# Order of the last weight loads in a fused decoder kernel: two down parts ahead of the embedding's gate weights, and a split emitted later

## The chip, the cores and the metric

The kernel runs on one core of a Trainium2 chip. Five engines of the core matter: PE (matrix products; its weight loads are listed as PEld), DVE and ACT (elementwise work), POOL (little here) and SP, which only issues transfers. Each engine works through its own queue of instructions in order; semaphores tie the queues together. The metric is the time of one execution in microseconds (us) on the device. "Slower" and "faster" are measured against the kernel before, on the same chip.

## The reference, cut to what matters

Two layers are computed for 256 tokens of width 1024 in float32. The last sub-layer of the second layer and what follows it are these lines:

```python
y = jnp.zeros(xf.shape, F32)
for e in range(N_EXPERTS):                       # 8 experts, top 2 of 8 for each token
    y = y + combine[:, e:e + 1] * swiglu(xf, w_gate_up[e], w_down[e]).astype(F32)
...
x = layer_norm(DEEPNORM_ALPHA * x + h, ln_ffn_g[i], ln_ffn_b[i])     # h is y
x = x + jax.nn.sigmoid(x @ ple_w_gate[i]) * (p[i] @ ple_w_proj[i])   # the gated embedding
```

An expert has 1024 x 7168 weights for gate and up and 3584 x 1024 for down, 44 MB in all; the eight make 352 MB. `ple_w_gate` has 4 MB for a layer, `ple_w_proj` 1 MB.

## The kernel before

**Experts.** `experts` goes over eight turns `e`, one expert each, sorted by how many tokens they got. Turn `e` handles `GR[e]` groups of 32 tokens; the last turn, 7, has two groups. The hidden width is cut into four quarters `q`. `gate_up(e, q)` makes a quarter's hidden values (eight tiles of weights of 1 MB; the last quarter is half as wide and has four), ACT and DVE apply the gate, `trans(e, q)` turns them (`hT`), and `down(e, q)` multiplies them with the down weights (four tiles of 1 MB; two for the last quarter). `down(e, q - 1)` stands behind `gate_up(e, q)`, so the last piece of the text is `gate_up(7, 3)`, `down(7, 2)`, `trans(7, 3)`, `down(7, 3)`. `trans(7, 3)` writes `hT`, which `down(7, 3)` reads.

**Ring.** Every weight tile is one turn of a ring of 22 buffers of 1 MB (`ringtile`, L785). `TURNS = "3p4p5p6p7ppp21089abcxx"` names the buffer of each turn: a digit or a to c is a buffer with its own tag, `p` is any of seven buffers that share one tag, `x` any of two that share another. The turn in `Finish.load` that takes `self.pw` is a first letter of the string. A turn waits until the work that read the buffer 22 turns before is done.

**The end.** `Finish` (L1233) does what follows the experts. `load` takes tiles for `ple_w_proj` (`pw`), for the split of p (`pTs`), and for the four pieces of `ple_w_gate` (`raws`; called gate loads 1 to 4 below), and issues these five loads. `prepare` splits a float32 weight into a high part (a cast on ACT) and a low part (a subtraction on DVE): twice for `pw`, twice for p (source `pT1`, made at the start of the experts' stage), and eight times for `raws` (called gate casts 1 to 8; two for each gate load). Between them stand the 24 products `p_part` of p with `ple_w_proj` on PE, which ACT copies away (`pp`). It also loads the norm's two vectors (`gb`). `end` gathers the last expert's result (`collect`), places and adds it, normalises, turns, and multiplies with the gate weights; it sends the output.

**Order.** The queues are laid down when the program is built, by a planner that plays the program through a model of the engines and the loads. Whenever an engine is free there, it takes the first instruction in the text that can begin; later text may overtake text that waits. Two things bind it. Inside `in_order` (all of `end`) an engine keeps the order of the text. And the tiles of one tag are handed out in the order in which their first writes stand in the text, also where a buffer would be free earlier. Tags that matter here: the seven `p` buffers, and `mis`, four banks of PSUM (`psM`), of which the last expert's sum holds one from `down(7, 0)` on, and of which `p_part`, `trans(7, 3)` and the turn of the placement matrix (`scatter`) take one each time they call `mis()`.

In the trace nearly every instruction carries line 90, the helper that records it; groups are told apart by the tiles' names. All ring tiles are named `raw`.

Of the kernel before, what the change touches and what calls it, by code (L numbers as in the profile page):

```python
# [19 lines left out]
P = 128  # L20
S = 256
D = 1024
NB = S // P
DFF = 2816
NE = 8
# [49 lines left out]
def trunk(ctx: ExitStack, tc: tile.TileContext, cst, x, p, ln_mix_g, ln_mix_b, ln_ffn_g, ln_ffn_b, ab_w_in,  # L75
          ab_b_f, ab_w_out, c_w_qkv, c_sinks, c_w_out, ffn_w_gate_up, ffn_w_down, router_w, router_b,
          moe_w_gate_up, moe_w_down, ple_w_gate, ple_w_proj, out):
    nc = tc.nc
# [50 lines left out]
    def mis():  # L129
        return psM.tile([P, 512], F32, tag="mis", name="mis")  # L130
# [44 lines left out]
    def rawtile(dt=F32):  # L175
        return rawp.tile([P, 2048], dt, tag="raw", name="raw", bufs=7)
# [163 lines left out]
    def p_part(prep, b, n, ac):  # L340
        pT, HL = prep
        for k in range(2):
            for j, (a, w) in enumerate(((0, 0), (0, 1), (1, 0))):
                T.matmul(ac, pT[b][:, a, k, :], HL[k][w][:, 512 * n:512 * (n + 1)],
                         start=(k == 0 and j == 0), stop=(k == 1 and j == 2))
        return ac
# [438 lines left out]
    def ringtile(dt=F32):  # L785

        i = TURNS[turn[0] % len(TURNS)]
        turn[0] += 1
        if i == "p":
            return rawtile(dt)  # L790
        if i == "x":
            return big.tile([P, 2048], dt, tag="xT", name="raw", bufs=2)
        return ring.tile([P, 2048], dt, tag="raw" + i, name="raw", bufs=1)
# [34 lines left out]
    def fetch_(dst, src):  # L828
        with after(queued[0]):
            queued[0] = nc.sync.dma_start(dst, src)  # L830
# [5 lines left out]
    def of_turn(w, e, static):  # L836

        if static or e == 0:
            return w[0, e]
        if not ids:  # L840
            for i in range(1, NE):
                with after(queued[0]):
                    ids[i] = nc.values_load(idi[0:1, i:i + 1], engines=[mybir.EngineType.SP], min_val=0, max_val=NE - 1)
        return w[0, bass.ds(ids[e], 1)].rearrange("o d f -> (o d) f")

    def load_gu(dst, e, q, k, s=slice(0, 2), static=False):
        wgu = of_turn(moe_w_gate_up, e, static).rearrange("(k p) (s n) -> p k s n", p=P, s=2)
        fetch_(dst, wgu[:, k, s, cols[q]])
# [7 lines left out]
    for b in range(NB):  # L856
# [5 lines left out]
        for k in range(8):  # L862
            q = T.matmul(ps[0:NE, 0:P], rw[:, k, :], t[:, 0, k, :], start=(k == 0), stop=(k == 7))
# [117 lines left out]
    def experts(rest, finish):  # L981
# [6 lines left out]
        items, raws = [], {}  # L988
# [3 lines left out]
                if e or q:  # L992
                    items += [(e - (q == 0), (q - 1) % 4, k) for k in range(chunks[q - 1])]
        items += [(NE - 1, 3, k) for k in range(chunks[3])]
        used, passed = [0], [None]

        def fetch(e, q, k, s=None):
            if s is None:
                if k % 2 == 0:
                    raws[0] = raw = ringtile()  # L1000
                    wd = of_turn(moe_w_down, e, rest).rearrange("(k p) n -> p k n", p=P)
                    step = 1 if e == NE - 1 and q == 3 and k == 2 else 2
                    for i in range(0, 2, step):
                        fetch_(raw[:, D * i:D * (i + step)].rearrange("p (k n) -> p k n", n=D),
                               wd[:, 8 * q + k + i:8 * q + k + i + step, :])
                return raws[0][:, D * (k % 2):D * (k % 2 + 1)]
            if q == 3:
                if k % 2 == 0:
                    raws[2] = t = ringtile()
                    for i in range(2):  # L1010
                        load_gu(t[:, D * i:D * (i + 1)].rearrange("p (s n) -> p s n", s=2), e, q, k + i, static=rest)
                return raws[2][:, D * (k % 2):D * (k % 2 + 1)]
            if s == 0:
                raws[2] = ahead.pop((q, k), None) if not rest and e == 0 else None
                if raws[2] is None:
                    raws[2] = ringtile()
                    load_gu(raws[2].rearrange("p (s n) -> p s n", s=2), e, q, k, static=rest)
            return raws[2][:, FQ * s:FQ * (s + 1)]

        def weights(*it):  # L1020
            assert items[used[0]] == it
            used[0] += 1
            return fetch(*it)

        def place_of(dst, e, b, n):

# [113 lines left out]
        def down(e, q):  # L1140
            n = gr[e]
            m = 2
            if q == 0:
                st[e]["y"] = [mis() for _ in range((n + 1) // 2)]
            y = [(st[e]["y"][g // 2][:, 256 * (g % 2):256 * (g % 2 + 1)], g % 2 == 0) for g in range(n)]
            hT = st[e]["hT%d" % q]
            for k in range(chunks[q]):
                W = weights(e, q, k)
                mm = side_by_side(y, [hT[:, g * m + k % m, k // m, :] for g in range(n)], W,
                                  q == 0 and k == 0, q == 3 and k == chunks[3] - 1)  # L1150
                if k == min(KT, chunks[q] - 1):
                    passed[0] = mm
# [8 lines left out]
        def ystile():  # L1161
            return moe.tile([P, D], F32, tag="ys", name="ys", bufs=1)
# [38 lines left out]
        for e in range(NE):  # L1201
            for q in range(4):
                gate_up(e, q, dict(zip(SC, scatter(e - 1))) if q == 1 and e else {})
                if not rest and e == 0 and q == 0:
                    gates()
                    turn_p()
                if not rest and e == 0 and q == 2:
                    gather((1,), xs)
                    keep_x()
                if e == NE - 1 and q == 3:  # L1210
                    finish.load()
                    finish.prepare()
                if q:
                    down(e, q - 1)
                elif e:
                    down(e - 1, 3)
                if q == 3 and e % 2 and e + 1 < NE:
                    gather((e + 1, e + 2), xk)
                trans(e, q)
                if e == NE - 1 and q == 3:  # L1220
                    scatter(e)[0](None)
        down(NE - 1, 3)
        ys = ystile()
        finish.end(functools.partial(collect, st[NE - 1]["y"], ys, gr[NE - 1]), ys, st[NE - 1]["pT"], CT * gr[NE - 1],
                   functools.partial(add, NE - 1))
# [3 lines left out]
    def turn_p():  # L1229
        for b in range(NB):  # L1230
            A.copy(pT1[:, b], tr4(pt1[:, b], 2)[:, :2 * P].rearrange("p (k t) -> p k t", t=P))

    class Finish:  # L1233


        def load(self):
            self.pw, self.pTs = ringtile(), ringtile(F32R)
            nc.sync.dma_start(self.pw.rearrange("p (k n) -> p k n", n=D), ple_w_proj[1].rearrange("(k p) n -> p k n", p=P))
            w = ple_w_gate[1].rearrange("(k p) n -> p k n", p=P)
            self.raws = []  # L1240
            for n in range(2):
                for k0 in (0, 4):
                    self.raws.append(ringtile())
                    nc.sync.dma_start(self.raws[-1].rearrange("p (k n) -> p k n", n=512),
                                      w[:, k0:k0 + 4, 512 * n:512 * (n + 1)])

        def parts(self, t, src):

            split(t[:, :D], t[:, D:], src)
            return t[:, :D], t[:, D:]  # L1250

        def prepare(self):

            pHL = [self.parts(ringtile(F32R), self.pw[:, D * k:D * (k + 1)]) for k in range(2)]
            pTs = self.pTs[:, :8 * P].rearrange("p (b a k t) -> p b a k t", b=NB, a=2, k=2)
            for b in range(NB):
                split(pTs[:, b, 0], pTs[:, b, 1], pT1[:, b])
            self.pp = ringtile().rearrange("p (b n) -> p b n", b=NB)
            for b in range(NB):
                for n in range(2):  # L1260
                    A.copy(self.pp[:, b, half[n]], p_part(([pTs[:, i] for i in range(NB)], pHL), b, n, mis()))
            self.HL = [[], []]
            for i in range(8):
                H, L = self.parts(ringtile(F32R), self.raws[i // 2][:, D * (i % 2):D * (i % 2 + 1)])
                for k in range(2):
                    sl = slice(512 * k, 512 * (k + 1))
                    self.HL[i // 4].append((H[:, sl], L[:, sl]))
            self.gb = ringtile()
            for i, v in enumerate((ln_ffn_g, ln_ffn_b)):
                nc.sync.dma_start(self.gb[:, D * i:D * (i + 1)], v[1:2, :].broadcast_to([P, D]))  # L1270
            x2t = ringtile().rearrange("p (b n) -> p b n", b=NB)
            self.x2 = [x2t[:, b, :] for b in range(NB)]
            self.xT = [ringtile(F32R).rearrange("p (a k t) -> p a k t", a=2, k=8) for b in range(NB)]
# [109 lines left out]
```

## Time and profile before

| what | value |
|---|---|
| runs (3) | 1373.24, 1374.14, 1376.18 us; median 1374.14 |
| the profiled execution | 1376.53 us, of it 1374.8 us from the first to the last instruction (the span) |
| busy PE / DVE / ACT / POOL | 1345.0 / 396.1 / 326.7 / 27.5 us |
| HBM read | 430.21 MB |

A row of a timeline has the start, the duration, the engine, the line, the operation, the tiles written and read, the shapes, the number of instructions, and in brackets the idle time of the engine before and what ended it. PE records two instructions for each float32 product with expert weights, so that one tile of down weights of the last turn makes 32. PEclk is the granted TensorE clock, 1.00 for 2.4 GHz and 0.50 for 1.2 GHz. All times in rows are counted from the span's start.

### The profile page before, as it was taken

How to read it: one execution, taken by the hardware profiler on the slowest of the kernel's cores; microseconds unless marked ns; L12 is line 12 of the kernel's file. 1: busy time of each engine (PE TensorE's matmuls, PEld its weight loads, DVE VectorE, ACT ScalarE, POOL GpSimd, SP SyncE). 2: the span in 40 equal slices, each digit the busy share in tenths (PEclk: the TensorE clock that was granted, in tenths of full speed). 3: DMA queues.
4: the chain of work that ended last, by engine and by line, in shares of the span. 5: the costliest groups of instructions: out<-in, count | busy, mean ns of one | idle time of the engine just before them, and what ended most of it. 6: DMA issues, size and time to landing. Idle time of an engine off the chain costs nothing. (4 is left out here: it accounts for less than half of the span.)

```text
span 1374.8 us, 37450 instructions
## 1 busy us (share of the span) xinstructions
PE 1345.0 (98%) x16967; PEld 891.3 (65%) x16967; DVE 396.1 (29%) x781; ACT 326.7 (24%) x618; POOL 27.5 (2%) x31
## 2 busy tenths in 40 slices
PE   8999999999999999999999999999999999999977
PEld 6786788888776666655556555665555665665546
DVE  5466654555877700010010011001010002002054
ACT  4545444443557100110010010011010001001041
POOL 0000300000000000000000000000000000000000
PEclk9999999999999999999999999999999999999988
DMA  9462564566581899999999999999999999999950
GB/s 323 160 204 74 162 204 138 168 223 198 174 325 68 318 403 405 384 399 400 408 408 401 407 407 392 407 406 392 407 408 395 399 408 406 389 408 407 377 224 34
DMA packets 143146, 433.77 MB, mean 316 GB/s; under 512 B 8834, under 2 KB 14978, under 8 KB 142978
## 3 DMA queue, kind: packets, MB, share of 16 engines
q1 hardware_dynamic: 142834, 431.22, 82.4%
q8 instruction: 135, 2.21, 0.7%
q14 instruction: 33, 0.27, 0.1%
q10 hardware_dynamic: 144, 0.07, 0.0%
HBM read 430.21 MB, written 1.05 MB: 314 GB/s over the span
## 5 line engine op out<-in xcount | busy, mean ns | idle before, releaser
L90 PE MATMUL acc<-raw,xg 128*32 128x256 f32 x9408 | 519.7, 380 | 0.0
L90 PEld LDWEIGHTS acc<-raw,xg 128*32 128x32 f32 x9408 | 300.9, 110 | 209.7 <-issue 11.3
L90 PE MATMUL mis<-raw,hT 128*32 128x256 f32 x4704 | 262.7, 379 | 2.1 <-DMA raw<-in_moe_w_down 2.1
L90 PE MATMUL acc<-H,xT 128*128 128x512 f32 (+2 forms) x768 | 227.8, 380 | 0.8 <-ACT xT L90 0.8
L90 DVE TENSOR_TENSOR h<-h,acc 128x512 f32<-128x512 f32 (+2 forms) x64 | 37.8, 596 | 638.1 <-PE acc L90 478.9
L90 PEld LDWEIGHTS mis<-raw,hT 128*32 128x32 f32 x4704 | 151.8, 110 | 103.7 <-DMA raw<-in_moe_w_down 2.7
L90 DVE TENSOR_TENSOR L<-raw,H 128x1024 fp32r<-128x1024 f32 (+2 forms) x134 | 151.2, 1135 | 110.2 <-ACT H L90 109.6
L90 ACT CAST H<-raw 128x1024 fp32r<-128x1024 f32 (+2 forms) x138 | 133.6, 975 | 147.4 <-PE acc L90 136.9
L90 PEld LDWEIGHTS acc<-H,xT 128*128 128x128 f32 x768 | 141.1, 192 | 29.0 <-ACT xT L90 1.7
L90 ACT ACTIVATE h<-acc 128x512 f32<-128x512 f32 (+2 forms) x64 | 32.9, 522 | 482.8 <-PE acc L90 482.8
L90 PE MATMUL acc<-L,xT 128*128 128x512 f32 (+2 forms) x384 | 141.3, 374 | 0.0
L90 PEld LDWEIGHTS acc<-L,xT 128*128 128x128 f32 x384 | 72.6, 189 | 13.8 <-DVE L L90 1.2
L90 ACT COPY hT<-mis 128x512 f32<-128x512 f32 (+2 forms) x47 | 21.7, 495 | 196.2 <-PE mis L90 195.9
L90 PE MATMUL acc<-H,hT 128*128 128x512 f32 x176 | 55.8, 396 | 0.0
L90 DVE SCALAR_TENSOR_TENSOR x<-mis,gateT,x 128x512 f32<-128x512 f32 x28 | 21.0, 751 | 92.4 <-PE mis L90 90.9
L90 PE MATMUL acc<-H,oT 128*128 128x512 f32 x128 | 43.8, 410 | 0.0
L90 PEld LDWEIGHTS acc<-H,hT 128*128 128x128 f32 x176 | 33.0, 187 | 8.0
L90 PE MATMUL acc<-L,hT 128*128 128x512 f32 x88 | 34.8, 395 | 0.0
L90 DVE COPY ys<-mis 32x256 f32<-32x256 f32 x42 | 17.8, 423 | 48.7 <-ACT ys L90 41.5
L90 PEld LDWEIGHTS mis<-c,h 128*128 128x128 f32 (+1 forms) x212 | 21.7, 140 | 14.0 <-issue 12.3
L90 PE MATMUL mis<-c,h 128*128 128x128 f32 (+1 forms) x212 | 30.1, 271 | 0.0
L90 PEld LDWEIGHTS acc<-H,oT 128*128 128x128 f32 x128 | 23.9, 188 | 7.0 <-issue 1.9
(209 smaller groups left out, 783.7 us busy)
## 6 DMA issues: line engine op xcount, KB each, us to landing
raw<-in_moe_w_gate_up SPq DMA_DIRECT2D x192, 1024.0 KB, 18.2
raw<-in_moe_w_down SPq DMA_DIRECT2D x111, 1024.0 KB, 17.0
raw<-in_moe_w_gate_up SPq DMA_DIRECT2D x64, 512.0 KB, 12.8
raw<-in_ffn_w_gate_up SPq DMA_DIRECT2D x20, 1024.0 KB, 5.2
raw<-in_ffn_w_down SPq DMA_DIRECT2D x10, 1024.0 KB, 5.2
raw<-in_ab_w_in SPq DMA_DIRECT2D x9, 1024.0 KB, 7.7
raw<-in_ple_w_gate SPq DMA_DIRECT2D x8, 1024.0 KB, 13.3
raw<-in_ab_w_out SPq DMA_DIRECT2D x4, 1024.0 KB, 5.2
```

The source lines that it names most:

```text
L90: self.last = getattr(self.eng, name)(*args, **kw)
```

## The change

In the last quarter of the last turn, `finish.load()` and `finish.prepare()` are taken apart. The new order of the text is: `gate_up(7, 3)`; `load_p` (`pw`, `pTs` and the load of `ple_w_proj`); the loads of all tiles of `down(7, 2)` and `down(7, 3)`, kept in `got` for the products that come later; `load` (the four gate loads and now `gb`); the products of `down(7, 2)`; `prepare_p` (the splits of `pw` and p, the 24 products, their copies); `trans(7, 3)` and the turn of the placement matrix; `down(7, 3)`; `prepare` (the eight gate splits, and the tiles that `end` writes); `end`. By the letters of the ring, in the order of the turns:

| | before | after |
|---|---|---|
| `pw`, `pTs` | 3 p | 3 p |
| `down(7, 2)`, `down(7, 3)` | last: x 3 p 4, p 5 | next: 4 p 5 p, 6 p |
| gate loads 1 to 4 | 4 p 5 p | 7 p p p |
| `gb` | a | 2 |
| two splits of `pw`, `pp` | 6 p, 7 | 1 0, 8 |
| gate splits 1 to 8 | p p p 2 1 0 8 9 | 9 a b c x x 3 p |

```diff
-        used, passed = [0], [None]
+        used, passed, got = [0], [None], {}
...
         def weights(*it):
             assert items[used[0]] == it
             used[0] += 1
-            return fetch(*it)
+            return got.pop(it) if it in got else fetch(*it)
...
                 if e == NE - 1 and q == 3:
+                    finish.load_p()
+                    for it in items[used[0]:]:
+                        got[it] = fetch(*it)
                     finish.load()
-                    finish.prepare()
                 if q:
                     down(e, q - 1)
                 elif e:
                     down(e - 1, 3)
+                if e == NE - 1 and q == 3:
+                    finish.prepare_p()
                 if q == 3 and e % 2 and e + 1 < NE:
                     gather((e + 1, e + 2), xk)
                 trans(e, q)
                 if e == NE - 1 and q == 3:
                     scatter(e)[0](None)
         down(NE - 1, 3)
+        finish.prepare()
...
-        def load(self):
+        def load_p(self):
             self.pw, self.pTs = ringtile(), ringtile(F32R)
             nc.sync.dma_start(self.pw.rearrange("p (k n) -> p k n", n=D), ple_w_proj[1].rearrange("(k p) n -> p k n", p=P))
+
+        def load(self):
             w = ple_w_gate[1].rearrange("(k p) n -> p k n", p=P)
...
+            self.gb = ringtile()
+            for i, v in enumerate((ln_ffn_g, ln_ffn_b)):
+                nc.sync.dma_start(self.gb[:, D * i:D * (i + 1)], v[1:2, :].broadcast_to([P, D]))
...
-        def prepare(self):
+        def prepare_p(self):
...
                     A.copy(self.pp[:, b, half[n]], p_part(([pTs[:, i] for i in range(NB)], pHL), b, n, mis()))
+
+        def prepare(self):
+
             self.HL = [[], []]
...
-            self.gb = ringtile()
-            for i, v in enumerate((ln_ffn_g, ln_ffn_b)):
-                nc.sync.dma_start(self.gb[:, D * i:D * (i + 1)], v[1:2, :].broadcast_to([P, D]))
```

## Rows read from the trace of the kernel before

**Rows 1.** The page, busy tenths in 40 equal slices of the span.

```profile
PE   8999999999999999999999999999999999999977
DMA  9462564566581899999999999999999999999950
```

**Rows 2.** Stretches: length, busy time of PE to POOL, clock, DMA share, GB/s.

```profile
1240.00:1260.00 20.00, 20.00 (x324) 11.15 (x320) 4.74 (x9) 3.72 (x9) 0.00 (x0) 1.00 1.03 408
...
1308.00:1316.00 8.00, 7.03 (x23) 5.16 (x24) 8.00 (x9) 8.00 (x12) 0.00 (x0) 0.79 0.84 307
...
1330.85:1342.91 12.06, 8.98 (x16) 4.05 (x16) 8.73 (x16) 2.04 (x5) 1.00 (x1) 0.58 0.00 0
```

**Rows 3.** Timeline of SP, issues at the end of the experts.

```profile
1287.67 0.62 SPq L1238 DMA_DIRECT2D raw<-in_ple_w_proj  x1
...
1303.28 14.80 SPq L830 DMA_DIRECT2D raw<-in_moe_w_down  x7
```

**Rows 4.** Size and time to landing of loads issued at 1286.3, 1290.3, 1317.7 us.

```profile
raw<-in_moe_w_gate_up SPq DMA_DIRECT2D x1, 512.0 KB, 10.7
...
raw<-in_ple_w_gate SPq DMA_DIRECT2D x1, 1024.0 KB, 14.7
...
raw<-in_moe_w_down SPq DMA_DIRECT2D x1, 512.0 KB, 11.9
```

**Rows 5.** Timeline of PE from the last gate and up quarter on.

```profile
1297.85 7.09 PE L90 MATMUL acc<-raw,xg 128*32 128x256 f32 x128
1308.79 1.48 PE L90 MATMUL mis<-raw 128*128 128x512 f32 x3 [3.84 <-ACT raw L90]
1310.45 6.03 PE L90 MATMUL mis<-raw 128*128 128x512 f32 x21 [0.19 <-DVE raw L90]
1316.64 1.93 PE L90 MATMUL mis<-raw,hT 128*32 128x256 f32 x32 [0.16 <-DMA raw<-in_moe_w_down]
...
1321.21 0.46 PE L90 MATMUL mis<-c,h 64*128 64x64 f32 x4
...
1327.19 3.66 PE L90 MATMUL mis<-raw,hT 128*32 128x256 f32 x64 [0.74 <-DMA raw<-in_moe_w_down]
...
1342.91 11.09 PE L90 MATMUL acc<-raw 128*128 128x512 f32 x40
```

**Rows 6.** Timeline of ACT over the same stretch.

```profile
1305.01 0.59 ACT L90 ACTIVATE h<-acc 64x512 f32<-64x512 f32 x1 [6.26 <-PE acc L90]
1305.50 2.92 ACT L90 CAST raw<-raw 128x1024 fp32r<-128x1024 f32 x3
1308.33 0.71 ACT L90 CAST raw<-pT 128x256 fp32r<-128x256 f32 x2
...
1326.57 0.37 ACT L90 COPY hT<-mis 128x256 f32<-128x256 f32 x1 [3.92 <-PE mis L90]
1330.91 0.74 ACT L90 COPY ys<-mis 32x256 f32<-32x256 f32 x2 [3.96 <-PE mis L90]
```

**Rows 7.** Timeline of PE, down parts of turn 6 (three groups) and of turn 7.

```profile
1197.72 10.54 PE L90 MATMUL mis<-raw,hT 128*32 128x256 f32 x192
...
1268.78 3.64 PE L90 MATMUL mis<-raw,hT 128*32 128x256 f32 x64
1272.34 0.66 PE L90 MATMUL mis<-c,h 128*128 128x128 f32 x4
1272.93 3.66 PE L90 MATMUL mis<-raw,hT 128*32 128x256 f32 x64
```

**Rows 8.** Timeline of DVE, splits of p and weights, and the end's norm.

```profile
1309.98 0.76 DVE L90 TENSOR_TENSOR raw<-pT,raw 128x256 fp32r<-128x256 f32 x2
1310.65 8.03 DVE L90 TENSOR_TENSOR raw<-raw 128x1024 fp32r<-128x1024 f32 x7
...
1331.67 0.86 DVE L90 COPY ys<-mis 32x256 f32<-32x256 f32 x2 [12.99 <-ACT ys L90]
...
1340.33 1.41 DVE L90 SCALAR_TENSOR_TENSOR raw<-raw,rs 128x512 f32<-128x512 f32 x2
```

## The prediction

> **What bounds the kernel now.** I read the page first, then the stretches, then the timelines of the last 80 us. The page shows PE and the loads both close to full from the middle of the span to slice 37 [rows 1]: in the experts' stage the loads run at 408 GB/s beside a PE that never rests [rows 2], so neither end says which one limits. The tail says it. The last gate and up quarter starts at 1297.85 and takes 7.09 us, so PE is through at 1304.94 [rows 5], while its last load, issued at 1286.3, has landed 10.7 us later, at 1297.0 [rows 4]. PE is behind the loads by 8 us there. Then PE stands still for 3.84 us, since the products of p wait for ACT [rows 5]; the loads of the down parts are issued only from 1303.28 on, behind those of the embedding, which began at 1287.67 [rows 3], and every tile of `down(7, 2)` starts within a load's landing [rows 5]. The last of them, issued at 1317.7, lands 11.9 us later, at 1329.6 [rows 4]; `down(7, 3)` ends at 1327.19 + 3.66 = 1330.85 [rows 5]. What follows (collect from 1330.91 [rows 6], norm, gate products from 1342.91 [rows 5], output) is a chain that starts from that point. So the change is worth what it does to the end of `down(7, 3)`, called D below, and to whatever the chain behind D still lacks then.
>
> **What the loads give.** The change moves 6 MB of down weights ahead of 4 MB of gate weights; no byte is added. At 408 GB/s a load of 1024 KB takes 1,048,576 / 408,000 = 2.57 us. The three loads from `pw` to gate load 2 landed between 1297.0 and 1290.3 + 14.7 = 1305.0, so 2.67 us each [rows 4]. With 2.6 us (between the two) from 1297.0 on: `pw` 1299.6, `down(7, 2)` 1302.2 to 1310.0, `down(7, 3)` 1315.2, gate loads 1 to 4 at 1317.8, 1320.4, 1323.0, 1325.6, the norm's vectors 1328. The bounds of 2.57 and 2.67 move gate load 2, the ninth, to 1320.1 and 1321.0. The buffers that these loads take were read long before: the furthest one is that of the seventh tile of `gate_up(7, 2)`. SP has no other work to be moved past.
>
> The Trainium skill ("DMA: Bandwidth & Descriptors", Specifications) gives a core some 358 GB/s from HBM. By it, as an estimate, a load would take 2.93 us and gate load 2 would land at 1323.4, 3 us later. The trace does not agree: 408 GB/s [rows 2].
>
> **What PE could gain.** With its weights there, `down(7, 2)` can start at 1304.94; four tiles of 1.93 us [rows 5], the last landed at 1310.0, end at about 1312. Taken alone this is worth up to 8 us of D.
>
> **Where it goes.** Between `down(7, 2)` and `down(7, 3)` the new text has `prepare_p`, then `trans(7, 3)`, then the turn of the placement matrix. `trans` takes a bank of the tag `mis`, and so do the products of p, which stand ahead of it in the text; so in PE's queue `trans(7, 3)` stands behind them, and `down(7, 3)` behind its copy. D now hangs on the products of p, and these on the casts of p on ACT.
>
> When do those casts stand in ACT's queue? They write `pTs`, one of the seven `p` buffers. In the trace of before they read `pT1`, made long before, and ACT sat idle for 6.26 us just ahead [rows 6]; yet they stand behind three weight casts. Being ready is not what places them: their buffer is handed out behind those of the gate loads with a `p`, whose first writes stand earlier in the text. In the new text this holds for three gate loads, 2, 3 and 4, that all have a `p`; the casts of p cannot be placed before gate load 4 has been issued in the planner's model.
>
> What has the model put on ACT by then? Its loads come just in time: in turn 7 the transposes sit in the middle of the down part (64, then 4, then 64 [rows 7]), where PE had found no landed tile, while in turn 6, with half as much more work for a tile, all 192 run through [rows 7]. With PE waiting tile by tile in the model, a tile lands there one or two issues after its own. When gate load 4 is issued, gate loads 1 and 2 are then landed, and ACT, which has nothing else, has been given gate casts 1, 2 and 3, likely 4. On the chip the queue is fixed. ACT comes to these casts at 1307.5 and stands there until gate load 1 lands at 1317.8 and gate load 2 at 1320.4, with the casts of p behind them.
>
> **The sum.** Gate load 2 at 1320.4; two casts at 2.92 / 3 = 0.97 us [rows 6] until 1322.3. From the start of the casts of p to the first product 0.46 us (1308.33 to 1308.79 [rows 5, 6]): 1322.8. The 24 products with their waits for DVE: 1308.79 to 1316.48, 7.69 us [rows 5]. I take it whole, its first part at the half clock too: it came after 3.84 us of idle PE, and the mean clock of 0.79 over 8 us means 3.4 us at 1.2 GHz, 1.7 us of work lost [rows 2]; now PE will have idled for 10 us before. 1330.5. `trans` 0.46 [rows 5], its copy and the step to `down(7, 3)` 1326.57 to 1327.19, 0.62 [rows 5, 6], and 0.1 between: 1331.7. `down(7, 3)` 3.66 [rows 5]: D at 1335.4, against 1330.85, so +4.5 us. Everything behind D keeps its length, as the gate splits are done by then (gate load 4 at 1325.6 and two splits) and as the clock behind D was low already (0.58 from D to the first gate product [rows 2]). The profiled execution has 1376.53 us and would have 1381.0; it lies 2.4 us above the median of the runs, and on the median the sum is 1374.14 + 4.5 = 1378.6 us.
>
> Costs taken as nothing: the moved issue of `gb` (needed at about 1339, there at 1328), the two splits of `pw` (ACT and DVE idle while PE does `down(7, 2)`; without that cover two casts of 0.97 us), the tiles that `end` writes (their buffers are those of `down(7, 2)`). Bounds: only three gate casts ahead, -1.0; loads -0.3 to +0.6; the clock low for twice those 3.4 us, +1.7, or not at all, -1.7. The likeliest case alone lies between 1376.9 (clock) and 1380.9 (clock and loads).
>
> **Rivals.**
>
> *The casts of p come at once* (the other side). If the planner gives `pTs` its buffer early, the products of p run from 1312 on and take 6 us; `trans` and copy 1.2, `down(7, 3)` 3.66: D at 1322.8, 8 us earlier. Not all of it stays: the eight gate splits, 8.03 / 7 = 1.15 us each on DVE [rows 8], 9.2 us in all, were done by 1318.7, with 12.99 us of idle DVE behind them [rows 8]; now gate load 4 lands at 1325.6, behind D, so that part of them falls between D and the end of the norm's first half (1340.33 + 1.41 = 1341.74, 10.9 us behind D [rows 8]). With all eight there and 3.2 us of gaps to take some, 2 us are left; with the first four done ahead of D, 6.6 us. Middle 4.3: 1369.8 us. For it: nothing that these casts read is late. Against it: their place in the queue of before [rows 6]. It decides if no gate cast stands ahead of the casts of p.
>
> *Only gate load 1's casts stand ahead.* The casts of p at 1317.8 + 1.9 = 1319.7, and by the same steps D at 1332.7, +1.9: 1376.0 us. For it: in the model gate load 2 lands only shortly before gate load 4 is issued.
>
> *Gate load 3's casts stand ahead too.* One load of 2.6 us more: D at 1338, 1381.2 us. Against it: a landing less than one issue after its own, where tiles took one to two.
>
> *The change does nothing*, since the bytes end at the same time (1328 for 1329.6) and the gate casts take the place of the down weights as the last to land: a gain of at most 3 us, in the first rival's bounds.
>
> **How the numbers follow.** Likeliest 0.60, first rival 0.20, only gate load 1 0.12, gate load 3 too 0.05, else 0.03. Within 0.2% (2.75 us, about what a measurement of this kernel tells from none) lie most of the second rival, a fifth of the first and a small part of the likeliest: 0.19. Faster: 0.17, the rest of the first and half of the unlisted. Slower: 0.64. The range goes from 1371.2, which leaves out the better part of the first rival, to 1381.0.
>
> **What would show it.** In the trace after: the last landing of down weights near 1315; `down(7, 2)` from 1305 to about 1312; then PE idle for some 10 us, ended by ACT; on ACT three or four gate casts, the first released by a load near 1318, ahead of the casts of p; the products of p from about 1323, a half clock in their first part; `down(7, 3)` ending near 1335 with no wait for a load. The prediction is wrong if the casts of p follow the splits of `pw` at about 1308, if `trans(7, 3)` stands ahead of the products of p, or if the gate loads land well before 1317.

## The result, and the profile after

The changed kernel is slower: a median of 1383.64 us over 4 runs (1382.62 to 1384.57) against 1374.56 over 4 runs of the kernel before, ratio 1.0065 with a 95% interval of 1.0048 to 1.0083. The forecast had the sign and the places; it had 1378.6 us and a range that ended at 1381.0. The profiled execution took 1384.36 us, 7.8 more than that of before.

From the changed kernel, SP's timeline, and the size and time to landing of the loads issued at 1287.0, 1300.0 and 1302.8 us (answering to [rows 3, 4]):

```profile
1289.80 11.29 SPq L830 DMA_DIRECT2D raw<-in_moe_w_down  x7
1301.20 14.15 SPq L1251 DMA_DIRECT2D raw<-in_ple_w_gate  x4
```

```profile
raw<-in_moe_w_gate_up SPq DMA_DIRECT2D x1, 512.0 KB, 10.7
...
raw<-in_moe_w_down SPq DMA_DIRECT2D x1, 512.0 KB, 16.4
...
raw<-in_ple_w_gate SPq DMA_DIRECT2D x1, 1024.0 KB, 18.9
```

The last piece of gate and up is there at 1297.7, the last down weights at 1316.4 instead of 1329.6, gate load 2 at 1321.7 instead of 1305.0. PE and then ACT over the same stretch (answering to [rows 5, 6]):

```profile
1304.78 5.36 PE L90 MATMUL mis<-raw,hT 128*32 128x256 f32 x96
1310.53 1.93 PE L90 MATMUL mis<-raw,hT 128*32 128x256 f32 x32 [0.38 <-DMA raw<-in_moe_w_down]
1324.20 8.40 PE L90 MATMUL mis<-raw 128*128 128x512 f32 x24 [11.74 <-ACT raw L90]
1332.53 0.46 PE L90 MATMUL mis<-c,h 64*128 64x64 f32 x4
...
1333.55 3.66 PE L90 MATMUL mis<-raw,hT 128*32 128x256 f32 x64
...
1349.21 11.48 PE L90 MATMUL acc<-raw 128*128 128x512 f32 x40
```

```profile
1305.53 1.98 ACT L90 CAST raw<-raw 128x1024 fp32r<-128x1024 f32 x2
1319.15 1.99 ACT L90 CAST raw<-raw 128x1024 fp32r<-128x1024 f32 x2 [11.65 <-DMA raw<-in_ple_w_gate]
1321.85 1.99 ACT L90 CAST raw<-raw 128x1024 fp32r<-128x1024 f32 x2 [0.71 <-DMA raw<-in_ple_w_gate]
1323.75 0.70 ACT L90 CAST raw<-pT 128x256 fp32r<-128x256 f32 x2
...
1333.12 0.38 ACT L90 COPY hT<-mis 128x256 f32<-128x256 f32 x1
```

Read the two together. `down(7, 2)` runs from 1304.78 to 1312.46 with one wait of 0.38 us; it began at 1316.64 in [rows 5]. Then PE stands for 11.74 us, and the row says for whom: ACT. ACT itself stands for 11.65 us for a gate load, casts the tiles of gate loads 1 and 2, and only then the two small ones of p (1323.75), whose source had long been there. The products of p begin at 1324.20, `trans(7, 3)` behind them at 1332.53, its copy `hT` at 1333.12, `down(7, 3)` at 1333.55 with no wait for a load: D, its end, is 1337.21, 6.36 us later than before.

Three stretches of the changed kernel: the idle one, the products of p, and D to the first gate product (columns as in [rows 2]):

```profile
1312.46:1324.20 11.74, 0.00 (x1) 0.00 (x0) 3.63 (x4) 4.34 (x6) 0.00 (x0) 0.65 0.97 366
1324.20:1332.60 8.40, 8.40 (x25) 6.10 (x26) 6.44 (x7) 5.76 (x8) 0.00 (x0) 0.68 0.22 85
1337.21:1349.21 12.00, 8.91 (x18) 3.99 (x17) 8.74 (x16) 2.04 (x5) 1.00 (x1) 0.61 0.00 0
```

The transfers stay busy while PE does nothing; the products then run at a mean clock of 0.68; the last row is 12.00 us long, as its counterpart in [rows 2] is 12.06.

### The profile page after: what moved, and what is told of

Same layout as the page of the kernel before. It is cut to its first block, busy times and chain, and to the rows that moved or that the text cites. A ratio compares the mean times of both kernels' runs of the same rounds, so it can differ in the third digit from the quotient of the medians.

```text
span 1382.6 us, 37451 instructions
## 1 busy us (share of the span) xinstructions
PE 1345.6 (97%) x16967; PEld 892.1 (65%) x16967; DVE 396.5 (29%) x781; ACT 327.1 (24%) x618; POOL 27.5 (2%) x31
## 6 DMA issues: line engine op xcount, KB each, us to landing
raw<-in_ple_w_gate SPq DMA_DIRECT2D x8, 1024.0 KB, 10.2
```

## The experiments

Two explanations are set against each other below. Queue theory: D waits for the casts of p, which stand behind gate casts in ACT's queue, and `trans(7, 3)` stands behind the products of p in PE's. Load theory: what costs is that the gate weights now land last, with their split behind them.

The columns: D and the start of the first gate product in the profiled execution, that execution's own time, the median of the runs, and the ratio to the kernel before on the same chip with its interval.

| kernel | D | gate product | profiled | median | ratio |
|---|---|---|---|---|---|
| before | 1330.85 | 1342.91 | 1376.53 | 1374.56 | |
| changed | 1337.21 | 1349.21 | 1384.36 | 1383.64 | 1.0065 [1.0048, 1.0083] |
| split_not_late | 1335.68 | 1347.65 | 1382.04 | 1382.04 | 1.0057 [1.0043, 1.0071] |
| split_late_alone | 1331.70 | 1342.50 | 1375.53 | 1376.81 | 1.0023 [1.0012, 1.0033] |
| gate_loads_sooner | 1332.64 | 1344.45 | 1377.77 | 1377.95 | 1.0036 [1.0022, 1.0049] |
| before_p_first | 1330.05 | 1342.01 | 1375.91 | 1374.10 | 1.0001 [0.9992, 1.0010] |
| p_first | 1327.05 | 1346.54 | 1379.81 | 1378.66 | 1.0029 [1.0020, 1.0039] |
| trans_first | 1316.67 | 1337.99 | 1372.42 | 1373.71 | 0.9997 [0.9988, 1.0006] |
| p_and_trans_first | 1321.68 | 1338.51 | 1371.32 | 1371.93 | 0.9985 [0.9976, 0.9994] |
| p_first_sooner | 1327.06 | 1342.64 | 1376.08 | 1374.86 | 1.0005 [0.9996, 1.0014] |
| p_and_trans_first_sooner | 1321.52 | 1336.75 | 1370.32 | 1371.34 | 0.9984 [0.9975, 0.9993] |
| before_again | 1330.22 | 1342.11 | 1375.55 | 1374.97 | 1.0004 [0.9995, 1.0013] |
| after_again | 1336.22 | 1348.29 | 1383.09 | 1382.90 | 1.0062 [1.0047, 1.0078] |
| pe_kept_busy | 1335.44 | 1347.52 | 1382.18 | 1380.40 | 1.0044 [1.0028, 1.0059] |

### Which half of the change costs

**split_not_late**: the new order of loads, both splits emitted where they stood.

```diff
                     finish.load()
+                    finish.prepare_p()
+                    finish.prepare()
...
-                if e == NE - 1 and q == 3:
-                    finish.prepare_p()
...
-        finish.prepare()
```

> The changed kernel, with both splits emitted where they stood before, ahead of down(7,2); only the order of the loads is changed. Queue theory: the same queues on ACT and PE as in the changed kernel, D at 1337, 1382 to 1385 us, ratio to before 1.005 to 1.008. Rival (the late split costs, since it puts gate casts between D and the norm): several us faster than the changed kernel, 1375 to 1380.

**split_late_alone**: the order of loads of before, the gate split emitted late.

```diff
                     finish.load_p()
-                    for it in items[used[0]:]:
-                        got[it] = fetch(*it)
                     finish.load()
+                    finish.prepare_p()
...
-                if e == NE - 1 and q == 3:
-                    finish.prepare_p()
```

> The order of loads of the kernel before, with the gate weights' split emitted behind the last down part, as the change has it. Queue theory: gate casts 1 to 4 ahead of the casts of p cost about 1 us there, since gate loads 1 and 2 land at 1302 and 1305, and D is set by the last landing of down weights: D at 1330.8, 1374 to 1376 us, ratio 0.999 to 1.001. Rival (emitting the split late costs by itself): 1378 or more.

The first came as the queue theory had it: the same queues on ACT and PE, the same wait, 1382.04. Where the text puts the splits makes no difference that these intervals can tell once the loads are in the new order. PE and ACT of split_not_late:

```profile
1322.63 8.44 PE L90 MATMUL mis<-raw 128*128 128x512 f32 x24 [11.28 <-ACT raw L90]
...
1332.02 3.66 PE L90 MATMUL mis<-raw,hT 128*32 128x256 f32 x64
```

```profile
1320.28 1.99 ACT L90 CAST raw<-raw 128x1024 fp32r<-128x1024 f32 x2 [0.71 <-DMA raw<-in_ple_w_gate]
```

The second missed: 0.999 to 1.001 was expected, 1.0023 came. The late split is not free in the old order either. PE of split_late_alone, and the stretch of its products:

```profile
1310.45 1.65 PE L90 MATMUL mis<-raw 128*128 128x512 f32 x3 [6.68 <-ACT raw L90]
...
1328.04 3.66 PE L90 MATMUL mis<-raw,hT 128*32 128x256 f32 x64 [0.49 <-ACT hT L90]
```

```profile
1310.45:1319.40 8.95, 8.70 (x28) 6.28 (x32) 5.92 (x7) 4.86 (x7) 0.00 (x0) 0.66 1.03 409
```

PE idles 6.68 us ahead of the products instead of 3.84 in [rows 5], as four gate casts stand ahead where one stood, and they take 8.95 us to the end of the last (1310.45 to 1319.40) instead of 7.69. That takes away the slack that the late loads had covered: `down(7, 3)` is now released by ACT's copy of `hT`, no longer by a load. This execution is the fastest of its eight, and its D lies only 0.85 us behind that of before; how the rest of the 2.8 us comes about (1376.81 for 1373.99 in the kernel before on that chip) isn't shown.

### Is it the wait of the casts of p, and of trans(7,3) behind the products?

**gate_loads_sooner**: the changed kernel, gate loads 1 and 2 issued ahead of the loads of `down(7, 3)`; `load(0)` issues these two, `load(1)` the other two and `gb`.

```diff
-                    for it in items[used[0]:]:
-                        got[it] = fetch(*it)
-                    finish.load()
+                    for n in range(2):
+                        for it in items[used[0]:]:
+                            if it[1] == 2 + n:
+                                got[it] = fetch(*it)
+                        finish.load(n)
```

> The changed kernel with one thing altered: gate loads 1 and 2 are issued between the loads of down(7,2) and those of down(7,3), that is 2 MB or 5.2 us sooner; the queues of ACT and PE are the same. Queue theory: the wait for gate load 2 is what holds the casts of p and with them D, so D moves one for one with that landing: gate load 2 at 1316.6, D at 1332 in place of 1337.2, 1377 to 1380 us, ratio to before 1.002 to 1.004. Load theory (the last landing of gate weights, 1327, and the split behind it set the end): nothing moves, 1382 to 1385 us.

1.0036, inside the expected interval, with the same queues. ACT and PE of gate_loads_sooner:

```profile
1314.81 1.99 ACT L90 CAST raw<-raw 128x1024 fp32r<-128x1024 f32 x2 [0.92 <-issue]
1316.70 0.71 ACT L90 CAST raw<-pT 128x256 fp32r<-128x256 f32 x2
1322.55 1.99 ACT L90 CAST raw<-raw 128x1024 fp32r<-128x1024 f32 x2 [5.13 <-DMA raw<-in_ple_w_gate]
```

```profile
1317.16 1.22 PE L90 MATMUL mis<-raw 128*128 128x512 f32 x2 [5.98 <-ACT raw L90]
...
1325.08 1.65 PE L90 MATMUL mis<-raw 128*128 128x512 f32 x6 [1.01 <-ACT raw L90]
...
1328.22 0.65 PE L90 MATMUL mis<-c,pm 128*64 128x128 f32 x4 [0.97 <-ACT raw L90]
1328.98 3.66 PE L90 MATMUL mis<-raw,hT 128*32 128x256 f32 x64
```

The casts of p come 7 us sooner than in the changed kernel, D only 4.6. The rest is lost to the same mechanism one step on: the copies of the products stand behind the casts of gate load 3 (1322.55, released by its landing), and the last products, whose banks these copies free, wait 1.01 us for ACT, the turn of the placement matrix another 0.97. That the time fell into the expected interval is in part luck: the casts of gate load 2 came at 1314.81, some 2 us sooner than expected (a landing at 1316.6), and D did not move one for one with them.

**p_first** and **before_p_first**: the split of p moved to where `ple_w_proj` is loaded, in the changed kernel and in the kernel before. **trans_first**: in the changed kernel, `prepare_p` moved behind `trans(7, 3)` and the turn of the placement matrix.

```diff
         def load_p(self):
...
+            pTs = self.pTv = self.pTs[:, :8 * P].rearrange("p (b a k t) -> p b a k t", b=NB, a=2, k=2)
+            for b in range(NB):
+                split(pTs[:, b, 0], pTs[:, b, 1], pT1[:, b])
...
```

```diff
-                if e == NE - 1 and q == 3:
-                    finish.prepare_p()
...
                 if e == NE - 1 and q == 3:
                     scatter(e)[0](None)
+                    finish.prepare_p()
```

> The changed kernel, with the split of p moved to where its weights are loaded, so that the buffer of its casts is handed out ahead of the gate weights'. Queue theory (casts of p behind gate casts on ACT, trans(7,3) behind the products of p on PE): the casts of p come before 1305, the products of p run inside down(7,2), D falls from 1337.2 to about 1323; the eight gate casts now come behind D, so that 2 to 6.6 us come back: 1369 to 1374 us, ratio to before 0.996 to 0.999. Load theory (what costs is that the gate weights land last, at 1327, with their split behind): D may fall, but the first gate product stays near 1349, and the time near that of the changed kernel, 1382 to 1385.

> The kernel before, its order of loads kept, with the split of p moved to where its weights are loaded. Queue theory: the products of p begin a microsecond earlier or more, but down(7,3) waits for the last landing of down weights, 1329.6, as before: D at 1330.8, 1374 to 1376 us, ratio 0.999 to 1.001. Rival (the place of the casts of p is worth the same in either order of loads): 3 us or more faster than before.

> The changed kernel, with the products of p emitted behind trans(7,3) and the turn of the placement matrix. Queue theory: the casts of p still stand behind four gate casts and come near 1323.8, but down(7,3) no longer waits for them: D is set by the last landing of down weights, 1316.4, and comes near 1318; the products of p then run from 1324.2 to 1332.5 and the norm's turns on PE stand behind them, so that the first gate product comes near 1336 to 1339: 1371 to 1374 us, ratio to before 0.996 to 0.999. Load theory: the time stays near that of the changed kernel, 1382 to 1385.

before_p_first came as the queue theory had it: the casts of p move to 1277.04, and nothing is gained, since down weights still land last there. PE of before_p_first, `down(7, 3)`:

```profile
1326.39 3.66 PE L90 MATMUL mis<-raw,hT 128*32 128x256 f32 x64 [0.80 <-DMA raw<-in_moe_w_down]
```

In the changed kernel the early casts take 10 us from D (1337.21 to 1327.05), so the place of the casts was what held it. But 1378.66 is 4.7 us above the highest that the queue theory gave, and slower than before. Stretch from D to the first gate product, ACT and PE of p_first:

```profile
1327.05:1346.54 19.49, 6.86 (x18) 3.18 (x17) 17.43 (x24) 9.71 (x13) 1.00 (x1) 0.62 0.01 3
```

```profile
1329.54 7.67 ACT L90 CAST raw<-raw 128x1024 fp32r<-128x1024 f32 x8
```

```profile
1344.75 1.97 PE L90 MATMUL mis<-c,raw 128*128 128x128 f32 x8 [10.12 <-DVE raw L90]
```

All eight gate casts now stand behind the collect's copies, at 1329.54, and all eight subtractions fall into the norm: DVE is busy for 17.43 of 19.49 us there, against 8.73 of 12.06 in [rows 2], and PE waits 10.12 us for it. So the load theory comes near in its number (the first gate product moves by 2.7 us only), but not in its reason. The last gate load was there at 1325.7 (issued at 1311.4, 14.3 us to landing), ahead of D, and ACT had been idle for 4.92 us before 1322.48; what holds the eight casts is their place behind the collect's copies in ACT's queue. Why the planner put them there no run shows. What D gains goes to DVE.

trans_first shows the same from the other side. PE of trans_first, and its stretch from D to the first gate product:

```profile
1313.01 3.66 PE L90 MATMUL mis<-raw,hT 128*32 128x256 f32 x64 [0.55 <-ACT hT L90]
...
1336.23 1.94 PE L90 MATMUL mis<-c,raw 128*128 128x128 f32 x8 [4.21 <-DVE raw L90]
```

```profile
1316.67:1337.99 21.32, 14.60 (x42) 8.69 (x41) 18.26 (x26) 12.47 (x19) 1.00 (x1) 0.75 0.35 133
```

With `trans(7, 3)` ahead of the products, D falls by 20.5 us, to 1316.67; the casts of p, at 1322.95, no longer matter for it. Of the 20.5 us, 11 reach the first gate product; DVE, busy for 18.26 of 21.32 us, holds the rest, and the time is that of the kernel before: 1373.71 lies inside the expected 1371 to 1374, the ratio of 0.9997 above the expected 0.996 to 0.999.

### Versions built on this

**p_and_trans_first** joins the two edits; **p_first_sooner** and **p_and_trans_first_sooner** add the order of gate_loads_sooner.

> The changed kernel's own order of loads, with the split of p early and the products of p emitted behind trans(7,3): the fastest version so far (1371.3) without its sooner gate loads. D near 1319 to 1320; all eight gate splits fall behind D and take DVE for 9.4 us inside the norm's first half, of which the sooner loads had spared four: first gate product near 1339 to 1341, 1373 to 1376 us, ratio 0.999 to 1.001. If the sooner gate loads bring nothing: 1371 to 1372.

> The order of loads of the first run of this call, with the split of p early and the products of p emitted ahead of trans(7,3), as in the changed kernel. Queue theory: D near 1322.5; half of the gate splits, which cost 7.5 us behind D with all eight there, are done ahead of it: 3.5 to 4 us faster than with the split of p early alone (1378.7), so 1374 to 1376, ratio 1.000 to 1.001.

> The order of loads of the run above, with the split of p early and the products of p emitted behind trans(7,3). Queue theory: nothing that down(7,3) needs stands behind a gate load; its own weights land at 1321.6, D at 1322.5; four gate splits are done ahead of D, four (4.7 us of DVE) fall behind it: first gate product near 1339, 1370 to 1372 us, ratio 0.997 to 0.998. Load theory: 1376 us or more, since half of the gate weights still land last.

With both edits the new order of loads pays, by some 2 us: 0.9985, and 0.9984 with the sooner gate loads, intervals that end at 0.9994 and 0.9993. p_and_trans_first came out faster than expected (1373 to 1376). Between each other the two can't be told apart, so that the 2 us or more expected of the sooner loads did not come. With `trans(7, 3)` behind the products (p_first_sooner) they brought the expected 3.8 us, and the kernel is back at the time of before; D, though, stayed at 1327.06 where 1322.5 was expected, and what was won lies behind it (15.58 us from D to the first gate product for 19.49 in p_first). The stretch from D to the first gate product in p_and_trans_first_sooner:

```profile
1321.52:1336.75 15.23, 7.36 (x17) 3.35 (x17) 13.11 (x20) 5.92 (x9) 1.02 (x1) 0.64 0.18 70
```

DVE is still the engine that fills it, 13.11 of 15.23 us.

### Where the rest of the size is

**before_again** and **after_again** are the two kernels unchanged. **pe_kept_busy** adds 40 matmuls ahead of the products of p, for the time in which PE idles.

```diff
+            ac = acc()
+            for i in range(40):
+                T.matmul(ac, pHL[0][0][:, :P], pHL[0][0][:, :512], start=(i == 0), stop=(i == 39))
             self.pp = ringtile().rearrange("p (b n) -> p b n", b=NB)
```

> The kernel before, unchanged, profiled a second time. The working took the 2.4 us by which its first profiled execution lay above the median of the runs as a constant of every profiled execution. If so, this one lies 2 to 3 us above the median again. If it is the spread of executions, this one lies anywhere between 1372 and 1377, and what lay above the median is found in the trace: a shorter time from the last gate and up quarter to D, or from D to the end.

> The changed kernel, unchanged, profiled a second time. 1382 to 1385 us; if the profiled execution of before was a slow one of its kind and that of after a usual one, the ratio comes out at 1.006 to 1.007 again, D lies 15 to 16 us behind the landing of gate load 2, and the span behind D is as in the first profile within 1.5 us.

> The changed kernel with 40 matmuls more, that multiply the split weights of p with themselves into a bank that nobody reads, emitted ahead of the products of p: PE is then busy for some 10 us of the 11.7 that it idles there. Queue theory: D still hangs on gate load 2 and the casts of p. Clock theory, for what is left over: without the idle stretch there is no half clock in the products of p; they take 6.9 us, as with trans(7,3) ahead of them, in place of 8.4, D comes 1.5 us sooner, and the time is 1381 to 1383 us. If the clock costs nothing here: 1383 to 1385.

The second profile of before lies 0.6 us above its median, not 2 to 3: the 2.4 of the first is no constant, and fits the spread of executions. That of after lies 0.2 above its median (0.7 the first time). In pe_kept_busy 25 of the added matmuls run ahead of and between the tiles of `down(7, 2)`, which ends at 1320.35 instead of 1312.46, so that PE is busy up to the products. Stretches of pe_kept_busy, those in which the changed kernel's PE idles and does the products of p:

```profile
1312.50:1324.21 11.71, 11.51 (x118) 6.93 (x110) 3.63 (x4) 4.36 (x6) 0.00 (x0) 1.00 0.97 362
1324.21:1330.83 6.62, 6.11 (x25) 4.43 (x26) 6.17 (x7) 5.62 (x8) 0.00 (x0) 1.00 0.24 95
```

With PE busy ahead of them, the products of p run at a clock of 1.00 and take 6.62 us; in the changed kernel 8.40 and 7.97 us (two profiles). The median falls by 2.5 us against after_again on the same chip (four runs of each, 1379.62 to 1382.18 and 1382.19 to 1383.14), to 1380.40 where 1381 to 1383 was expected: a kernel that does more work is faster. The Trainium skill ("TensorE: Matmul & The Clock Gate", What's actually happening) says that a throttled clock is the default and that activity releases it. The trace agrees: 0.65 and 0.68 in the changed kernel with its idle PE, 1.00 here.

## Why the prediction was right in its mechanism and wrong in its size

**What the loads give.** Right in its order, and 1.3 us short. At 2.6 us each the ninth load behind the last gate and up piece was to land at 1320.4; it landed at 1321.7, 0.7 of it because the whole sequence was that much later in this execution (1297.7 for 1297.0), 0.6 because a load took 2.67 us, the upper bound given. In split_not_late, with the same queues, ACT took up gate load 2 at 1320.28.

**What PE could gain.** Right: `down(7, 2)` ended at 1312.46, forecast 1312.

**Where it goes.** Right in each point: four gate casts stood ahead of the casts of p on ACT, `trans(7, 3)` stood behind the products of p, PE idled for 11.74 us (some 10 forecast) and ACT ended it. gate_loads_sooner, p_first and trans_first each take away one link, and D falls by 4.6, 10.2 and 20.5 us. That the casts of p stood late because of where their buffer's first write stands in the text is borne out by p_first and before_p_first, where they run at 1276.83 and 1277.04; the times in the planner's model, from which the prediction got the number of casts ahead, are in no run. The Trainium skill ("PSUM — Partial Sum Buffer", Engine vs sequencer instructions) calls ACT's queue strictly first in, first out, and has matmuls start in program order. The trace agrees: the casts of p wait behind the second gate load's, and `trans(7, 3)` behind the last product.

**The sum** failed, in three terms, that make up the 5.0 us between 1378.6 and 1383.64: a step taken as a constant, a landing and a clock sized by those of before, and an end taken as unchanged.

- *The profiled execution against the median*, 1.7 us. "It lies 2.4 us above the median of the runs" was taken over to the changed kernel. Its profiled execution lay 0.7 above its median. (0.4 us of the term is before's own median, 1374.14 over three runs and 1374.56 over four.) The step from the one to the other is not a constant of the kernel, and it had no part in the range.
- *D*, 1.8 us: 1337.2 for 1335.4. It is gate load 2's landing (1.3) and the products of p (8.40 for 7.69; 0.7), less 0.2 in small steps. "I take it whole, its first part at the half clock too" priced the clock as [rows 2, 5] had it: 0.79 as the mean, behind 3.84 us of idle PE. Here it was 0.68 as the mean over the products, behind 11.74 us. The length of the idle stretch doesn't set the price: 8.95 us at 0.66 behind 6.68 us in split_late_alone, 7.97 us behind 12.37 in after_again. The clock was one of the bounds (1.7 either way), but the middle was put where before had stood, and the 1.7 was too much on the fast side: at 1.00 the products took 6.62 us, 1.1 less than in before.
- *Behind D*, 1.5 us: 1384.36 - 1337.21 = 47.15 for 1376.53 - 1330.85 = 45.68. "Everything behind D keeps its length" holds to the first gate product (12.00 for 12.06). What follows took 1.5 us more. In the second profiles it is 46.87 for 45.33. The traces say where. SP's last issue of output in the changed kernel, and then in the kernel before:

```profile
1375.92 0.33 SPq L1315 DMA_DIRECT2D out<-raw  x1
```

```profile
1369.27 0.33 SPq L1305 DMA_DIRECT2D out<-raw  x1
```

From the first gate product to this issue it is 26.71 for 26.36 us; from the issue to the end of the span (1382.6 and 1374.8) 6.68 for 5.53. So 1.15 of the 1.5 lie behind all that the engines compute. In the second profiles DVE's last addition comes 26.41 for 26.77 us after the first gate product, and 6.60 for 4.92 us remain; over the fourteen profiles of this case these last microseconds vary from 4.9 to 6.7. No experiment was made on that part, and why it is longer stays open.

The outcome lay 2.6 us beyond the end of the range. The bounds of the terms were all put around D; the spread of executions and the length of the end were taken as known.

**The first rival** (the casts of p come at once, 1369.8 us) did not happen, but p_first put its condition in place, and its price was wrong by 9 us: D came to 1327.05 and not 1322.8, and the gate splits cost 7.4 us behind D (19.49 for 12.06) where 1.4 to 6.0 had been given (2 to 6.6 of the 8 us were to be left). D is later because `down(7, 2)` and the products, which p_first's PE does by turns, were through at 1322.37 and not at 1318: PE waited 1.65 us for ACT ahead of them, and was busy with them for 15.85 us, at a mean clock of 0.89, where some 13 had been given. With it, too, the kernel ends on the slow side (1.0029). That PE would wait for DVE there was seen, but the cover that was counted on, idle DVE ahead of D, is of no use to casts that stand behind the collect on ACT.

**What stays open.** Of the 2.5 us that pe_kept_busy gives back, 1.4 to 1.8 are in the products; the profiles don't show where the rest is. Its profiled execution is the slowest of its four and lies only 0.9 us below that of after_again.

## What to carry to other kernels

A load that is moved ahead moves others back; ask first which instructions read those, and what stands behind them in the same in-order queue, however ready it is. Taking the wait away is not enough where the late weights still have to be prepared: look at the engine that prepares them (DVE here) in the stretch where that work will now fall. And a step between a profiled execution and the median of the runs is a term with a spread of its own, here half as large as the effect that was forecast (2.4 of 4.5 us).

## What the runs showed of the hardware

Forty matmuls whose result nobody reads made the changed kernel 2.5 us faster (1380.40 for 1382.90, four runs of each); the granted clock stayed at 1.00 through a stretch where it had been 0.65, and in the products behind it, where it had been 0.68. And executions of one program differ by up to 4.5 us (1371.65 to 1376.10 in 24 runs of the kernel before), more than the effect of most edits here; with 8 to 11 runs of a kernel the interval came down to 0.1% either way.
